# A hybrid transformer layer on one core: the gates take two or three turns over the contraction, the later conditioning keeps a pace, and the modulation moves to ScalarE

## The chip, the cores and the metric

The kernel runs on one core of a Trainium2 chip. The metric is the time of one execution in device microseconds (us); lower is better. A core has TensorE (PE in the profile) for matmuls and transposes, VectorE (DVE) and ScalarE (ACT) for work on whole tiles, GpSimd (POOL) for small things, and SyncE (SP), whose queue issues the loads from memory. Each engine runs its own instructions in order and waits on semaphores for the others.

## The reference, cut to what matters

256 latent tokens and 256 context tokens of width 2048 are normalised, modulated by the conditioning, and go through one input projection. Two attentions follow; their outputs are weighted by sigmoid gates, projected, and added to the tokens; a gated feed-forward network ends the layer.

```
sh1, sc1, g1, sh2, sc2, g2 = ada_terms(cond_lat, w_ada, b_ada)       # silu(c) @ w_ada + b_ada
ctx_terms = ada_terms(cond_ctx, w_ada, b_ada)
z_ctx = modulate(rms_norm(ctx, norm1_g), ctx_terms[0], ctx_terms[1])  # h * (1 + scale) + shift
ctx_proj = z_ctx @ w_in[:, :1088]          # MLA kv latent 512 | rope key 64 | GQA k 256 | GQA v 256
z_lat = modulate(rms_norm(x, norm1_g), sh1, sc1)
lat_proj = z_lat @ w_in                    # the same 1088 | MLA q latent 768 | GQA q 1024 | gates 2 x 2048
x = x + g1 * attend_and_merge(lat_proj, keys)    # sigmoid(g_a) * (o_a @ w_br_a) + sigmoid(g_b) * (o_b @ w_br_b), then @ w_out
x = x + g2 * conv_ffn(modulate(rms_norm(x, norm2_g), sh2, sc2))
```

## The kernel before, in words

**Products.** All large products are float32 in two parts: a high part, rounded, and a low part, the rest. `mm3` takes three matmuls for one product: high by high, high by low, low by high. Weights come by SP's queue, 1 MB at a time, into a ring of four buffers (`raw`). ACT casts the high part (`hi`), DVE subtracts to get the low one (`lo`), and three buffers hold such units; `take()` keeps two of them ahead of TensorE.

**Who goes when.** TensorE's order is the order in which the program is written. Side work stands in "lanes", generators that a modelled clock lets run a step at a time when the main line yields: class `Pace` adds up the modelled TensorE time, lets the modelled backlog of DVE, ACT and DMA run down with it, and runs a lane's next step when the backlogs are under that lane's limit. `Engine` holds the modelled cost of an instruction. `finish(lane)` runs what is left of a lane at once, whatever the backlog. On DVE and ACT the instructions then stand in an order that follows the model.

**Input projection.** The 16 tiles of 128 rows of the contraction are taken in parts (`CHUNKS`). For each part `gemv_chunk` makes the shift and scale from `w_ada` on TensorE (matmuls `raw,cs`, an ACT copy, a few transposes, three small DVE instructions on `md`), and `make_z` the modulated tokens: the high part by one ACT instruction, the modulated value by a DVE `tensor_scalar` in place (`sX<-sX,md`), the low part by a DVE subtraction. Latent tokens are `ZL`, context tokens `ZC`. Then blocks of columns are multiplied: a (MLA kv latent, rope key), b (GQA k and v), c (MLA q latent), d (GQA q) and the gates 0 to 3 of 1024 columns each; a and b take both kinds of token, the others latents alone. A block's result is copied out of PSUM by ACT the first time and added to what stands there by DVE (`sG<-bank,sG`, `sK<-bank,sK`) every later time. Two strings, `ORDER0` and `ORDERM`, set the order of blocks in a part; in the last two parts the gates come last and take both parts in one turn.

**Side work in this stretch.** `lane_ctx` prepares the context tokens in part 0. `ada_rest`, the later conditioning, makes shift, scale and gate for the rest of the layer on DVE: eight sums of 16 steps `acc<-raw,cs,acc`, each step half of a 1 MB load of `w_ada`; it may take 32 loads at first, then 48, then 64. In the last part `prep_b` rotates GQA keys and queries on DVE (`scratch<-sK,sY`, then `sK<-scratch`), turns them by transposes on TensorE (`ident,sK`) and splits them. It is finished when gate 0 is through. Then `lane_heads_b` (GQA attention) and `lane_latents` run as lanes under the gates 1 to 3, and `lane_latents` is finished after gate 3, ahead of `q_up`. It consists of `prep_cq`, `prep_ckv` (sums of squares by matmuls with `ones`, a reciprocal root on POOL, its spread over rows by `ident,rr`, and a scaling of four tiles on DVE) and `prep_kpe` (the rope key: transposes of `acc_pe`, a rotation on `kr` and `kt`, then eight transposes `ident,scratch`).

**Later stages.** q_up, the GQA projection, MLA attention, its projection, `w_out`, then the residual with the gate `g1`, which `ada_rest` makes (`acc,ones` matmuls and an ACT copy), the normalised tokens by transposes, up and down projection.

Of the kernel before, what the change touches and what calls it, by code (L numbers as in the profile page):

```python
# [29 lines left out]
CHUNKS = (2, 3, 3, 4, 4)  # L30
# [4 lines left out]
ORDER0, ORDERM, CTX_AT = "cd012ab3", "abcd0123", 2  # L35
# [3 lines left out]
REST_CI, REST_AFTER, REST_DMA = 1, 6.0, 6.0  # L39
GAPS = (0.0, 4.0, 10.0, 14.0, 14.0)  # L40
# [10 lines left out]
class Pace:  # L51
# [26 lines left out]
    def tick(self):  # L78
        if self.busy:
            return  # L80
        self.busy = True
        moved = True
        while moved:
            moved = False
            for lane in list(self.lanes):
                gen, ready, limit, dma, _ = lane
                if self.pe < ready or self.left["dve"] > limit or self.left["act"] > limit or self.left["dma"] > dma:
# [31 lines left out]
class Engine:  # L119
# [31 lines left out]
def _build(tc, nc, es, a):  # L151
# [139 lines left out]
    def lane_tables():  # L291

        r = slot("X0", [P, 4, P])
# [124 lines left out]
    def make_z(ci, cnd):  # L418
        kt0, nk = starts[ci], CHUNKS[ci]
        md = mods[ci]  # L420
        zt = slot(("ZL", "ZC")[cnd] + str(ci % 2), [P, 2, nk, T], F32R)
        zs[ci][cnd] = zt
        c = slice(cnd * T, (cnd + 1) * T)
        for k in range(nk):
# [8 lines left out]
    zs = [[None, None] for _ in CHUNKS]  # L433
# [7 lines left out]
    def ada_rest():  # L441
        for vname, v, gslot in (("sh2", 3, None), ("sc2", 4, None), ("g1", 2, "K1"), ("g2", 5, "Y0")):
            for sec in range(2):
# [4 lines left out]
                for j0 in range(0, 16, 2):  # L448
                    r = load(w_ada[:, j0:j0 + 2, c0:c0 + 1024], [P, 2, 1024])
                    taken_raws[0] += 1  # L450
                    for j in range(2):
# [3 lines left out]
                        else:  # L455
                            DVE.scalar_tensor_tensor(out=acc, in0=r[:, j, :], scalar=cs[:, j0 + j, 0:1], in1=acc,
                                                     op0=ALU.mult, op1=ALU.add)
                        yield 0.0
# [37 lines left out]
    rest = ada_rest()  # L496
# [46 lines left out]
    def zk(zt, k):  # L543
        return zt[:, 0, k, :], zt[:, 1, k, :]

# [3 lines left out]
    def block_a(ci):  # L549
        kt0, nk, z = starts[ci], CHUNKS[ci], zs[ci]  # L550
# [4 lines left out]
        for kk in range(nk):  # L555
            wh, wl = take()
            for n in range(5):
                m = 128 if n < 4 else 64
                for cnd in range(2):
                    zh, zl = zk(z[cnd], kk)  # L560
                    mm3(ps[n][:m, cnd * T:(cnd + 1) * T], wh[:, n * P:n * P + m], wl[:, n * P:n * P + m],
                        zh, zl, kk == 0 and cnd == 0, kk == nk - 1)
# [3 lines left out]
    def block_b(ci):  # L566
        kt0, nk, z = starts[ci], CHUNKS[ci], zs[ci]
# [3 lines left out]
        for k0, kn in halves(nk):  # L571
            wh, wl = take()
            for k in range(kn):
                kk = k0 + k
                for t in range(4):
                    c = slice((t % 2) * P, (t % 2 + 1) * P)
                    zh, zl = zk(z[t // 2], kk)
                    mm3(ps[t], zh[:, c], zl[:, c], wh[:, k, :], wl[:, k, :], kk == 0, kk == nk - 1)
# [3 lines left out]
    def block_c(ci):  # L582
        kt0, nk, z = starts[ci], CHUNKS[ci], zs[ci]
# [3 lines left out]
        for kk in range(nk):  # L587
            group_T(ps, take(), zk(z[0], kk), kk == 0, kk == nk - 1)
# [3 lines left out]
    def block_d(ci):  # L592
        kt0, nk, z = starts[ci], CHUNKS[ci], zs[ci]
# [3 lines left out]
        for kk in range(nk):  # L597
            wh, wl = take()
            zh, zl = zk(z[0], kk)
            for t in range(2):  # L600
                c = slice(t * P, (t + 1) * P)
                for n in range(2):
                    d = slice(n * 512, (n + 1) * 512)
                    mm3(ps[2 * t + n], zh[:, c], zl[:, c], wh[:, d], wl[:, d], kk == 0, kk == nk - 1)
# [9 lines left out]
    def block_g(cis, g):  # L614
# [4 lines left out]
        for i, (ci, k) in enumerate(ks):  # L619
            group_T(ps, take(), zk(zs[ci][0], k), i == 0, i == len(ks) - 1)  # L620
# [24 lines left out]
    def weights():  # L645
# [11 lines left out]
        for ci in range(nch):  # L657
            for b in order(ci):
                yield from wb(ci) if b == "b" else win(ci, *cols[b])
        for g in "0123":  # L660
            for ci in (nch - 2, nch - 1):
                yield from win(ci, *cols[g])
# [59 lines left out]
    for ci in range(nch - 1):  # L722
# [4 lines left out]
        if ci == REST_CI:  # L727
            pace.add(rest, after=REST_AFTER, limit=REST_LIM, dma=REST_DMA, prio=9)
        if ci == 2:
            pace.add(lane_tables(), after=5.0, limit=1.0, prio=8)  # L730
        for i, b in enumerate(order(ci)):
# [8 lines left out]
            run(block_g([ci], int(b)) if b in "0123" else {"a": block_a, "b": block_b, "c": block_c, "d": block_d}[b](ci))  # L740
# [4 lines left out]
    zo, zl_ = f"ZL{nch % 2}", f"ZL{last % 2}"  # L745
# [27 lines left out]
    def prep_b():  # L773
# [25 lines left out]
        qbh = slot("X0", [P, 4, 512], F32R)  # L799
# [192 lines left out]
    pace.limit(rest, REST_LIM_B)  # L992
# [6 lines left out]
    for g in range(4):  # L999
        run(block_g([last - 1, last], g))  # L1000
# [54 lines left out]
    pace.limit(rest, REST_LIM_Q)  # L1055
# [24 lines left out]
    obh = slot(zl_, [P, H, T], F32R)  # L1080
# [17 lines left out]
    oah = slot(zl_, [P, H, T], F32R)  # L1098
# [66 lines left out]
    pace.limit(rest, REST_LIM_A)  # L1165
# [4 lines left out]
    pace.limit(rest, REST_LIM_W)  # L1170
# [309 lines left out]
```

## Time and profile before

| | before |
|---|---|
| median of 3 runs | 1548.19 us (1545.66 to 1550.21) |
| the profiled execution | 1547.03 us, its span 1545.2 us |
| TensorE busy | 1506.1 us (97%) |
| DVE busy | 1103.3 us (71%) |
| ACT busy | 768.9 us (50%) |
| loads and stores | 350.44 MB, 227 GB/s in the mean |

The span is the part of the execution in which the profiler saw the core's engines at work; 1.8 us lie around it. Busy time is time in which an engine has an instruction under way; a TensorE matmul starts before the one ahead of it has ended, so its busy time says little about its speed, and its idle time (39 us) is what a wait costs. A wait is written behind the instruction that it held up, with the engine that ended it. Line L140 is the call in `Engine` through which all DVE and ACT work goes, L210 the matmul of `mm`, L219 the transpose, L398 the matmul of `gemv_chunk`.

### The profile page before, as it was taken

How to read it: one execution, taken by the hardware profiler on the slowest of the kernel's cores; microseconds unless marked ns; L12 is line 12 of the kernel's file. 1: busy time of each engine (PE TensorE's matmuls, PEld its weight loads, DVE VectorE, ACT ScalarE, POOL GpSimd, SP SyncE). 2: the span in 40 equal slices, each digit the busy share in tenths (PEclk: the TensorE clock that was granted, in tenths of full speed). 3: DMA queues.
4: the chain of work that ended last, by engine and by line, in shares of the span. 5: the costliest groups of instructions: out<-in, count | busy, mean ns of one | idle time of the engine just before them, and what ended most of it. 6: DMA issues, size and time to landing. Idle time of an engine off the chain costs nothing.

```text
span 1545.2 us, 23200 instructions
## 1 busy us (share of the span) xinstructions
PE 1506.1 (97%) x9361; PEld 1321.8 (86%) x9361; DVE 1103.3 (71%) x1553; ACT 768.9 (50%) x1145; POOL 14.2 (1%) x23
## 2 busy tenths in 40 slices
PE   6999999999999999999989999999999999999997
PEld 5788888899998988998879888888888888888885
DVE  3457686798778888698878989667666666555556
ACT  4634242355775446643446545555545555444444
POOL 0000000010000000000000000000000000000000
PEclk9999999999999999999989999999999999999998
DMA  9779888755346885478967878655555565555552
GB/s 360 243 251 331 286 313 292 257 181 191 110 134 208 280 286 187 146 275 310 351 225 257 295 256 294 215 182 181 186 192 191 167 204 180 194 199 196 195 195 78
DMA packets 123676, 350.44 MB, mean 227 GB/s; under 512 B 6718, under 2 KB 20264, under 8 KB 117040
## 3 DMA queue, kind: packets, MB, share of 16 engines
q1 hardware_dynamic: 123568, 348.96, 65.2%
q8 instruction: 73, 1.20, 0.3%
q14 instruction: 35, 0.29, 0.1%
HBM read 346.84 MB, written 2.10 MB: 226 GB/s over the span
## 4 chain that ended last, share of the span: by engine, by line
PE 92%; DVE 3%; DMA 3%; ACT 1%; issue 0%; SPq 0%; ACTq 0%; POOLq 0%; POOL 0%; DVEq 0%
PE bank L210 89%; PE bank L219 2%; PE bank L398 2%; DMA raw<-in_w_ada 1%; DMA raw<-in_w_in 1%; DVE scratch L140 1%; DVE lo L140 1%; DVE sK L140 1%; DMA sK<-in_x 0%; DVE sX L140 0%; ACT scratch L140 0%; DVE acc L140 0%; SPq L392 0%; ACT sK L140 0%; DVE sG L140 0%
## 5 line engine op out<-in xcount | busy, mean ns | idle before, releaser
L140 DVE TENSOR_TENSOR lo<-raw,hi 128x1024 fp32r<-128x1024 f32 (+2 forms) x463 | 548.5, 1188 | 302.6 <-ACT hi L140 300.7
L140 ACT CAST hi<-raw 128x1024 fp32r<-128x1024 f32 (+2 forms) x463 | 471.7, 1021 | 579.0 <-PE bank L210 471.1
L210 PE MATMUL bank<-sZL,hi 128*128 128x256 f32 (+2 forms) x2528 | 592.9, 316 | 3.0 <-ACT hi L140 2.5
L210 PE MATMUL bank<-sZL,lo 128*128 128x256 f32 (+1 forms) x1648 | 467.5, 284 | 0.6 <-DVE lo L140 0.6
L210 PEld LDWEIGHTS bank<-sZL,hi 128*128 128x128 f32 (+1 forms) x2528 | 422.2, 192 | 44.5 <-issue 7.5
L210 PEld LDWEIGHTS bank<-sZL,lo 128*128 128x128 f32 (+1 forms) x1648 | 315.6, 191 | 1.1 <-DVE lo L140 1.1
L210 PE MATMUL bank<-sX,hi 128*128 128x512 f32 (+1 forms) x896 | 287.6, 367 | 0.0
L210 PE MATMUL bank<-hi,sZC 128*128 128x512 f32 (+1 forms) x816 | 261.1, 383 | 0.0
L210 PE MATMUL bank<-sX,lo 128*128 128x256 f32 x704 | 198.0, 281 | 0.0
L210 PEld LDWEIGHTS bank<-sX,hi 128*128 128x128 f32 x896 | 164.8, 189 | 30.2 <-issue 0.5
L210 PEld LDWEIGHTS bank<-hi,sZC 128*128 128x128 f32 x816 | 152.6, 188 | 29.8
L140 DVE SCALAR_TENSOR_TENSOR acc<-raw,cs,acc 128x1024 f32<-128x1024 f32 x120 | 153.6, 1280 | 11.4 <-DMA raw<-in_w_ada 10.5
L210 PEld LDWEIGHTS bank<-sX,lo 128*128 128x128 f32 x704 | 133.4, 189 | 0.5 <-issue 0.5
L210 PE MATMUL bank<-lo,sZC 128*128 128x512 f32 (+1 forms) x344 | 131.5, 382 | 0.3 <-DVE lo L140 0.3
L210 PEld LDWEIGHTS bank<-lo,sZC 128*128 128x128 f32 x344 | 64.7, 188 | 13.2 <-DVE lo L140 0.7
L140 DVE TENSOR_TENSOR sK<-bank,sK 128x512 f32<-128x512 f32 (+1 forms) x92 | 60.0, 685 | 8.8 <-PE bank L210 7.5
L210 PE MATMUL bank<-hi,sZL 128*128 128x512 f32 x192 | 63.4, 393 | 0.1
L140 ACT COPY scratch<-bank 128x256 f32<-128x256 f32 (+3 forms) x92 | 35.1, 392 | 36.5 <-PE bank L210 23.1
L210 PE MATMUL bank<-sZC,hi 128*128 128x256 f32 x256 | 50.4, 284 | 1.4 <-DVE sZC L140 1.4
L210 PE MATMUL bank<-lo,sX 128*128 128x512 f32 x128 | 50.1, 392 | 0.9 <-DVE lo L140 0.9
L210 PE MATMUL bank<-hi,sX 128*128 128x512 f32 x128 | 50.3, 393 | 0.0
L140 DVE TENSOR_TENSOR sG<-bank,sG 128x512 f32<-128x512 f32 x64 | 41.9, 683 | 6.3 <-PE bank L210 6.3
(202 smaller groups left out, 1405.7 us busy)
## 6 DMA issues: line engine op xcount, KB each, us to landing
raw<-in_w_up SPq DMA_DIRECT2D x88, 1024.0 KB, 5.1
raw<-in_w_ada SPq DMA_DIRECT2D x82, 1024.0 KB, 6.7
raw<-in_w_down SPq DMA_DIRECT2D x44, 1024.0 KB, 5.8
raw<-in_w_in SPq DMA_DIRECT2D x37, 1024.0 KB, 5.1
raw<-in_w_out SPq DMA_DIRECT2D x16, 1024.0 KB, 7.5
raw<-in_w_ada SPq DMA_DIRECT2D x16, 768.0 KB, 5.1
raw<-in_w_br_b SPq DMA_DIRECT2D x8, 1024.0 KB
raw<-in_w_br_a SPq DMA_DIRECT2D x8, 1024.0 KB, 8.1
```

Source lines behind the costliest of these rows:

```text
L140: return f(*args, **kw)
L210: PE.matmul(out, lhsT, rhs, start=start, stop=stop, skip_group_check=True)
L219: PE.transpose(out, src, ident[:n, :n])
L398: PE.matmul(ps[32 * g:32 * g + 32, :cols], cs[:, j0 + jj, :], w[:, jj, :], start=j0 + j == 0, stop=j0 + j == 14, skip_group_check=True)
```

## The change

The parts become 2, 2, 4, 4, 4 tiles. The order of blocks is written out for each part, and a gate is multiplied over all parts since its last turn: gates 0 and 1 in three turns (part 0; 1 and 2; 3 and 4), gates 2 and 3 in two (0 to 2; 3 and 4), where each took four. So that a gate can reach back, the modulated latents of earlier parts are kept in four slots (`ZL0`, `ZL1`, `X0`, `ZL0` again), and some other tiles change their slot. In `make_z` the in-place modulation becomes a second ACT instruction, in all but the latents of part 0. `ada_rest` starts in part 2, not in part 1, and later in it (`REST_AFTER`), and is paced: as long as it has made fewer than one step for each `REST_EVERY` us of modelled TensorE time, its limit is raised to `REST_LATE`. The modelled costs become larger.

```diff
-CHUNKS = (2, 3, 3, 4, 4)
+CHUNKS = (2, 2, 4, 4, 4)
-ORDER0, ORDERM, CTX_AT = "cd012ab3", "abcd0123", 2
+ORDERS, CTX_AT = ("cd01ab", "abcd", "abcd2301", "abcd", "bdca0123"), 2
-REST_CI, REST_AFTER, REST_DMA = 1, 6.0, 6.0
-GAPS = (0.0, 4.0, 10.0, 14.0, 14.0)
+REST_CI, REST_AFTER, REST_DMA, REST_EVERY, REST_LATE = 2, 30.0, 6.0, 4.4, 2.6
+GAPS = (0.0, 4.0, 5.0, 14.0, 14.0)
...
             if self.key == "act":
-                c = 0.1 + 0.85e-3 * n
+                c = 0.17 + 0.86e-3 * n + (0.19 if "accum_out" in kw else 0.0)
...
             elif name in ("tensor_scalar", "tensor_copy"):
-                c = 0.06 + 0.58e-3 * n
+                c = 0.13 + 0.66e-3 * n
             else:
-                c = 0.06 + 1.05e-3 * n
+                c = 0.14 + 1.06e-3 * n
...
-        pace.tensor(n * 0.417e-3 if rhs.dtype == F32R else max(n, 256) * 1.67e-3)
+        pace.tensor(0.013 + n * 0.417e-3 if rhs.dtype == F32R else max(n, 256) * 1.67e-3)
...
-            ACT.activation(zt[:, 0, k, :], x, AF.Identity, bias=s2, scale=s1)
-            DVE.tensor_scalar(out=x, in0=x, scalar1=s1, scalar2=s2, op0=ALU.mult, op1=ALU.add)
-            DVE.tensor_sub(zt[:, 1, k, :], x, zt[:, 0, k, :].bitcast(F32))
+            hi, lo = zk(ci, cnd, k)
+            ACT.activation(hi, x, AF.Identity, bias=s2, scale=s1)
+            if ci == 0 and cnd == 0:
+                DVE.tensor_scalar(out=x, in0=x, scalar1=s1, scalar2=s2, op0=ALU.mult, op1=ALU.add)
+            else:
+                ACT.activation(x, x, AF.Identity, bias=s2, scale=s1)
+            DVE.tensor_sub(lo, x, hi.bitcast(F32))
...
+    def paced(limit):
+        def now():
+            if rest_from[0] is None:
+                rest_from[0] = pace.pe
+            return max(limit, REST_LATE) if rest_steps[0] < (pace.pe - rest_from[0]) / REST_EVERY else limit
+
+        return now
...
-    def order(ci):
-        if ci == nch - 1:
-            return "bdca"
-        o = ORDER0 if ci == 0 else ORDERM
-        return "".join(x for x in o if x in "abcd") if ci == nch - 2 else o
+    def gate_parts(ci, g):
+
+        done = [c for c in range(ci) if g in ORDERS[c]]
+        return list(range(done[-1] + 1 if done else 0, ci + 1))
...
-    pace.limit(rest, REST_LIM_B)
+    pace.limit(rest, paced(REST_LIM_B))
...
-        run(block_g([last - 1, last], g))
+        run(block_g(gate_parts(last, str(g)), g))
```

**Order, first place: the end of the gates, ahead of q_up, on TensorE.** `sZL` by `hi` or `lo` are matmuls of a gate, `sK,sX` those of a GQA head, the rows with `ones`, `rr`, `acc_pe` and `scratch` belong to `lane_latents`, `sZC` is q_up. Before:

```order
L210 MATMUL bank<-sZL_2968,lo 128x256
L219 MATMUL bank<-ident,acc_pe 128x64 x4
L210 MATMUL bank<-sZL_2968,hi 128x256 x2
L210 MATMUL bank<-sZL_2968,lo 128x256
...
L219 MATMUL bank<-ident,scratch 128x128 x8
L210 MATMUL bank<-sZC_4647,hi 128x256
```

And in the change:

```order
L215 MATMUL bank<-sZL_2772,lo 128x256
L215 MATMUL bank<-sK_4991,sX_3339 128x256 x12
L215 MATMUL bank<-ones,scratch 128x1 x8
L215 MATMUL bank<-ident,rr 128x128 x4
L224 MATMUL bank<-ident,acc_pe 128x64 x4
L224 MATMUL bank<-ident,scratch 128x128 x8
L215 MATMUL bank<-sZC_5050,hi 128x256
```

Before, the rows with `ones` and `rr` stand far ahead of this place, and sixteen rows of gate matmuls lie between the last two transposes of the lane. In the change the whole lane from its sums on stands behind the last gate matmul, with nothing between. What DVE has there in the change, from the root's spread (`rr`) to what the last transposes read (`sZL` and `sK` are low parts, `sK_604` to `sK_607` the four tiles that are scaled):

```order
L145 COPY rr<-st 128x128 x2
L145 TENSOR_TENSOR sZL_5474<-sY_4130,sZL_5473 128x256
...
L145 COPY kr<-bank 128x256
L145 SCALAR_TENSOR_TENSOR scratch<-sK_604,vec,scratch 128x512
L145 SCALAR_TENSOR_TENSOR scratch<-sK_605,vec,scratch 128x512
L145 SCALAR_TENSOR_TENSOR scratch<-sK_606,vec,scratch 128x512
L145 TENSOR_TENSOR sK_5102<-scratch,sK_5099 128x512
...
L145 TENSOR_TENSOR kt_5127<-kr,tabA 128x64
...
L145 CAST scratch<-kr 128x4x64 x2
L145 TENSOR_TENSOR scratch<-kr,scratch 128x4x64
```

Before, DVE had the scaling of those four tiles ahead of `COPY kr<-bank` among the low parts of the gates' weights.

**Second place: the end of gate 0 in the last set, on TensorE.** `ident,sK_710` are the transposes of the keys, `ident,sK_311` those of the queries. Before, the last of them:

```order
L219 MATMUL bank<-ident,sK_311 128x128 x4
L210 MATMUL bank<-sZL_2968,hi 128x256 x2
...
L219 MATMUL bank<-ident,sK_311 128x128 x12
L210 MATMUL bank<-sZL_2189,hi 128x256 x2
```

And in the change:

```order
L215 MATMUL bank<-sZL_2772,lo 128x256
L224 MATMUL bank<-ident,sK_710 128x128 x8
L224 MATMUL bank<-ident,sK_311 128x128 x16
L215 MATMUL bank<-sX_1702,hi 128x256 x2
```

All 24 transposes now stand behind gate 0 in one piece. On DVE the rotations of the queries (`sK_311<-scratch` ends one; `sX_3761` and `sX_3763` are low parts of turned keys and queries) stand in the change as follows:

```order
L145 TENSOR_TENSOR sX_3761<-bank,sX_3761 128x512 x2
L145 TENSOR_TENSOR sK_311<-scratch 128x512
L145 TENSOR_TENSOR scratch<-sK_311,sY_102 128x8x32 x2
L145 TENSOR_TENSOR scratch<-sK_311,sY_102 128x512
L145 TENSOR_TENSOR sX_3763<-bank,sZL_3762 128x512
L145 TENSOR_TENSOR sK_311<-scratch 128x512
L145 TENSOR_TENSOR sX_3763<-bank,sZL_3762 128x512
L145 TENSOR_TENSOR scratch<-sK_311,sY_102 128x8x32 x2
L145 TENSOR_TENSOR lo<-raw,hi 128x1024
L145 TENSOR_TENSOR sK_311<-scratch 128x512
```

Ahead of the last of these `sK_311<-scratch` DVE has 58 steps `acc<-raw,cs,acc` where it had 27 before, 8 additions `sG<-bank,sG` where it had 32, and 2 `tensor_scalar` on `sX` where it had 32.

**Third place: from part 1 to part 2, on ScalarE.** `scratch<-bank` is the copy of the conditioning's sums, `sZL` and `sZC` by `md` the high parts, `sX` by `md` the modulation in place, which stood on DVE before. In the change:

```order
L145 COPY scratch<-bank 128x512
L145 ACTIVATE sZL_1055<-sX_105,md 128x256 x2
L145 ACTIVATE sX_105<-sX_105,md 128x256 x2
L145 ACTIVATE sZL_1055<-sX_105,md 128x256 x2
L145 ACTIVATE sX_105<-sX_105,md 128x256 x2
L145 ACTIVATE sZC_1068<-sX_105,md 128x256 x2
L145 ACTIVATE sX_105<-sX_105,md 128x256 x2
L145 ACTIVATE sZC_1068<-sX_105,md 128x256 x2
L145 ACTIVATE sX_105<-sX_105,md 128x256 x2
```

On TensorE block b of part 1, the transposes of the conditioning and the first product of part 2 follow each other there with no gate between; before, gates 0 to 3 stood between the parts, gate 3 alone between parts 0 and 1.

## Rows read from the trace of the kernel before

**Rows 1.** The page's first part: busy us, share of span, instructions of each engine.
```profile
PE 1506.1 (97%) x9361; PEld 1321.8 (86%) x9361; DVE 1103.3 (71%) x1553; ACT 768.9 (50%) x1145; POOL 14.2 (1%) x23
```

**Rows 2.** TensorE's waits: line waited for, us in total, times, longest.
```profile
PE bank L219 <- DVE scratch L140: 9.6, 3, 5.9
...
PE bank L210 <- DVE lo L140: 2.5, 4, 0.9
...
PE bank L210 <- DVE sZC L140: 1.4, 1, 1.4
```

**Rows 3.** Windows: length, busy of PE, PEld, DVE, ACT, POOL; clock, DMA share, GB/s.
```profile
130.00:350.00 220.00, 219.65 (x1562) 193.35 (x1561) 172.74 (x257) 83.14 (x145) 5.98 (x3) 1.00 0.77 270
```

**Rows 4.** Another such window, the fullest in loads.
```profile
750.00:775.00 25.00, 25.00 (x112) 20.74 (x111) 22.73 (x20) 8.75 (x9) 0.00 (x0) 1.00 0.97 370
```

**Rows 5.** DVE's groups by form: count, busy us, mean ns, idle before.
```profile
L140 DVE TENSOR_TENSOR lo<-raw,hi 128x1024 fp32r<-128x1024 f32 x417 | 508.4, 1223 | 277.1 <-ACT hi L140 275.3
L140 DVE SCALAR_TENSOR_TENSOR acc<-raw,cs,acc 128x1024 f32<-128x1024 f32 x120 | 153.6, 1280 | 11.4 <-DMA raw<-in_w_ada 10.5
L140 DVE TENSOR_TENSOR sG<-bank,sG 128x512 f32<-128x512 f32 x64 | 41.9, 683 | 6.3 <-PE bank L210 6.3
...
L140 DVE TENSOR_SCALAR sX<-sX,md 128x256 f32<-128x256 f32 x32 | 12.1, 409 | 2.0 <-ACT sZL L140 2.0
```

**Rows 6.** Timeline between parts 0 and 1: start, us, instruction, count, [idle before]: DVE, ACT.
```profile
83.87 0.17 DVE L140 SCALAR_TENSOR_TENSOR md<-md,vec 128x6 f32<-128x6 f32 x1
...
85.91 0.75 DVE L140 TENSOR_TENSOR sZL<-sX,sZL 128x256 fp32r<-128x256 f32 x2
...
84.46 1.58 ACT L140 ACTIVATE sZL<-sX,md 128x256 fp32r<-128x256 f32 x3
```

**Rows 7.** Timeline, ends of the query rotations and their transposes: DVE, PE.
```profile
340.23 1.36 DVE L140 TENSOR_TENSOR scratch<-sK,sY 128x256 f32<-128x256 f32 x3
341.51 0.69 DVE L140 TENSOR_TENSOR sK<-scratch 128x512 f32<-128x512 f32 x1
...
353.32 0.67 DVE L140 TENSOR_TENSOR sK<-scratch 128x512 f32<-128x512 f32 x1
...
363.18 1.28 DVE L140 TENSOR_TENSOR sX<-bank,sX 128x512 fp32r<-128x512 f32 x2
...
370.81 1.47 PE L219 MATMUL bank<-ident,sK 128*128 128x128 f32 x12
```

**Rows 8.** Timeline of the latents' lane under the last gates: PE, POOL, DVE.
```profile
454.39 0.95 PE L210 MATMUL bank<-ones,scratch 128*128 128x1 f32 x8
...
455.71 1.01 POOL L239 TENSOR_TENSOR st<-st,mhalf 128x4 f32<-128x4 f32 x1 [17.94 <-ACT hi L140]
...
456.76 0.36 DVE L140 COPY rr<-st 128x128 f32<-128x128 f32 x2 [1.21 <-POOL st L239]
...
460.46 2.07 DVE L140 SCALAR_TENSOR_TENSOR scratch<-sK,vec,scratch 128x512 f32<-128x512 f32 x3
462.45 1.29 DVE L140 TENSOR_TENSOR sK<-scratch,sK 128x512 fp32r<-128x512 f32 x2
...
472.80 0.42 DVE L140 TENSOR_TENSOR kt<-kr,tabA 128x64 f32<-128x64 f32 x3
...
477.05 1.06 PE L219 MATMUL bank<-ident,scratch 128*128 128x128 f32 x8 [2.52 <-DVE scratch L140]
```

**Rows 9.** Timeline at the end of w_out: PE, DVE.
```profile
776.47 1.88 PE L210 MATMUL bank<-acc,ones 128*128 128x512 f32 x4
784.25 0.69 PE L219 MATMUL bank<-ident,scratch 128*128 128x128 f32 x2 [5.90 <-DVE scratch L140]
...
778.15 0.69 DVE L140 TENSOR_TENSOR scratch<-bank,sK 128x512 f32<-128x512 f32 x1 [1.70 <-ACT sK L140]
...
783.11 0.69 DVE L140 TENSOR_TENSOR sK<-sK,scratch 128x512 f32<-128x512 f32 x1
```

**Rows 10.** The clock at that end, in the windows' columns.
```profile
782.00:793.00 11.00, 7.08 (x30) 6.19 (x31) 8.42 (x19) 4.91 (x9) 1.11 (x2) 0.53 0.30 101
```

More of the change, by code (lines that the diff above doesn't have):

```diff
@@ L291, in lane_tables @@
     def lane_tables():
-        r = slot("X0", [P, 4, P])
+        r = scratch([P, 4, P])
         POOL.memset(r, 0.0)
@@ L420, in make_z @@
         md = mods[ci]
-        zt = slot(("ZL", "ZC")[cnd] + str(ci % 2), [P, 2, nk, T], F32R)
-        zs[ci][cnd] = zt
+        if cnd:
+            zc[ci] = slot(f"ZC{ci % 2}", [P, 2, nk, T], F32R)
+        elif kt0 % 4 == 0:
+            zl.append(slot(ZSLOTS[kt0 // 4], [P, 2, 4, T], F32R))
         c = slice(cnd * T, (cnd + 1) * T)
@@ L427, in make_z, with zk @@
             s1, s2 = md[:, 1, k, cnd:cnd + 1], md[:, 0, k, cnd:cnd + 1]
-            ACT.activation(zt[:, 0, k, :], x, AF.Identity, bias=s2, scale=s1)
-            DVE.tensor_scalar(out=x, in0=x, scalar1=s1, scalar2=s2, op0=ALU.mult, op1=ALU.add)
-            DVE.tensor_sub(zt[:, 1, k, :], x, zt[:, 0, k, :].bitcast(F32))
-            yield 0.0
-    zs = [[None, None] for _ in CHUNKS]
+            hi, lo = zk(ci, cnd, k)
[5 more added lines that the diff above has]
+            DVE.tensor_sub(lo, x, hi.bitcast(F32))
+            yield 0.0
+    ZSLOTS = ("ZL0", "ZL1", "X0", "ZL0")
+    zl, zc = [], {}
+    def zk(ci, cnd, k):
+        if cnd:
+            return zc[ci][:, 0, k, :], zc[ci][:, 1, k, :]
+        kt = starts[ci] + k
+        return zl[kt // 4][:, 0, kt % 4, :], zl[kt // 4][:, 1, kt % 4, :]
     s2col = cst.tile([P, KT], F32, name="s2col")
@@ L549, in block_a @@
     def block_a(ci):
-        kt0, nk, z = starts[ci], CHUNKS[ci], zs[ci]
+        nk = CHUNKS[ci]
         if ci == 0:
@@ L559, in block_a @@
                 for cnd in range(2):
-                    zh, zl = zk(z[cnd], kk)
+                    zh, zl_ = zk(ci, cnd, kk)
                     mm3(ps[n][:m, cnd * T:(cnd + 1) * T], wh[:, n * P:n * P + m], wl[:, n * P:n * P + m],
-                        zh, zl, kk == 0 and cnd == 0, kk == nk - 1)
+                        zh, zl_, kk == 0 and cnd == 0, kk == nk - 1)
             yield
@@ L566, in block_b @@
     def block_b(ci):
-        kt0, nk, z = starts[ci], CHUNKS[ci], zs[ci]
+        nk = CHUNKS[ci]
         if ci == 0:
@@ L582, in block_c @@
     def block_c(ci):
-        kt0, nk, z = starts[ci], CHUNKS[ci], zs[ci]
+        nk = CHUNKS[ci]
         if ci == 0:
@@ L587, in block_c @@
         for kk in range(nk):
-            group_T(ps, take(), zk(z[0], kk), kk == 0, kk == nk - 1)
+            group_T(ps, take(), zk(ci, 0, kk), kk == 0, kk == nk - 1)
             yield
@@ L592, in block_d @@
     def block_d(ci):
-        kt0, nk, z = starts[ci], CHUNKS[ci], zs[ci]
+        nk = CHUNKS[ci]
         if ci == 0:
@@ L657, in weights @@
         for ci in range(nch):
[L658 to L662, printed above, removed]
+            for b in ORDERS[ci]:
+                if b == "b":
+                    yield from wb(ci)
+                else:
+                    for c in gate_parts(ci, b) if b in "0123" else [ci]:
+                        yield from win(c, *cols[b])
         for u in range(2):
@@ L727, in _build @@
         if ci == REST_CI:
-            pace.add(rest, after=REST_AFTER, limit=REST_LIM, dma=REST_DMA, prio=9)
+            pace.add(rest, after=REST_AFTER, limit=paced(REST_LIM), dma=REST_DMA, prio=9)
         if ci == 2:
             pace.add(lane_tables(), after=5.0, limit=1.0, prio=8)
-        for i, b in enumerate(order(ci)):
+        for i, b in enumerate(ORDERS[ci]):
             if ci == 0 and i == CTX_AT:
@@ L739, in _build @@
                 lc = None
-            run(block_g([ci], int(b)) if b in "0123" else {"a": block_a, "b": block_b, "c": block_c, "d": block_d}[b](ci))
+            run(block_g(gate_parts(ci, b), int(b)) if b in "0123" else {"a": block_a, "b": block_b, "c": block_c, "d": block_d}[b](ci))
         while ci + 1 not in mods:
@@ L744, in _build @@
     last = nch - 1
-    zo, zl_ = f"ZL{nch % 2}", f"ZL{last % 2}"
+    zo, zn = "ZL1", "ZL0"
     run(block_b(last))
@@ L1053, in lane_q @@
             yield 0.0
-    pace.limit(rest, REST_LIM_Q)
+    pace.limit(rest, paced(REST_LIM_Q))
     run(q_up(0))
@@ L1163, in lane_a @@
             yield from head_a(2 * pr + par)
-    pace.limit(rest, REST_LIM_A)
+    pace.limit(rest, paced(REST_LIM_A))
     la = [pace.add(lane_a(i), limit=LIM_ATT, prio=1 + i) for i in range(2)]
@@ L1169, in _build @@
     hold[0] = 48
-    pace.limit(rest, REST_LIM_W)
+    pace.limit(rest, paced(REST_LIM_W))
     mgh = [slot(f"X{i}", [P, 8, T], F32R) for i in range(2)]
```

23 lines of the change are left out of this document (12 added, 11 removed).

## The prediction, made before the changed kernel ran

> **What bounds the kernel now.** I read the page's engine totals first, then TensorE's waits, the windows by stage, the groups of DVE, and last the timeline where the order of instructions changes. TensorE is busy for 1506.1 us [rows 1] of a span of 1545.2; it bounds the kernel, and only some 39 us of idling can be won at all. The list of its waits shows how few they are: transposes that read a DVE result wait 9.6 us in three places, the worst 5.9; products that wait for a low part 2.5 us in four [rows 2]. Through most of the projection it stands almost never: 219.65 of 220 us busy from 130 to 350 us, at full clock, with DVE busy 172.74 and loads at 270 GB/s [rows 3]. There, whatever makes DVE or ACT cheaper wins nothing by itself. A change can gain only at the few joints where TensorE waits, and it can lose at any place where side work stops having matmuls over it.
>
> **The change part by part.** The matmuls stay the same in number; what moves is which work lies over which.
>
> *Fewer gate additions, modulation off DVE.* 24 of 64 additions of 683 ns go, 16.4 us, and 30 of 32 `tensor_scalar` of 409 ns, 12.3 us [rows 5]. They lie under matmuls [rows 3], so I count them at nothing. ACT takes 30 instructions more; three high parts in a row take it 1.58 us, 0.5 each [rows 6], 15 us in all, also mostly under matmuls, but not at the joints, next.
>
> *Joint of parts 0 and 1.* Gate 3 covered it; now the first product of part 1 follows the transposes of the conditioning. Behind these come three small `md` instructions (0.17 each, 0.6 with their gaps), then on ACT two latent high parts, two in-place modulations, two context high parts and two more modulations, 0.5 each. The first tile's low part for context needs the seventh, 0.6+3.5, and a subtraction of 0.4 (0.75 for two) [rows 6]: 4.5 us. TensorE has for it part of a conditioning vector and the first latent products, some 1.5 to 2. I take +2.5 (2 to 3).
>
> *Joint of parts 1 and 2.* The same with four tiles; and the ACT copy of the conditioning's sums stands ahead, 0.6. The first context high part is the ninth ACT instruction and its low part needs the eleventh: 0.6+0.6+11x0.5+0.4 = 7.1, and two low parts of weights wait in the same DVE queue, which brings it to 7.85. TensorE covers 3 of it: +4.85. The low bound is 0, if the conditioning is far enough ahead. Here a page speaks against the edit: the Trainium skill, ScalarE: Activation LUTs, section Rules for kernel authors, gives simple arithmetic such as `mul` and `add` to VectorE rather than ScalarE. The rows agree on one instruction (409 ns on DVE [rows 5], 0.5 spaced on ACT [rows 6]); by that rule the joint would cost about 3.1, since two engines would share the chain.
>
> *Rest of the front.* The context tokens lose two `tensor_scalar` ahead of their low part: the 1.4 us wait for `sZC` [rows 2] falls by 0.7. Waits of 0.9 at part 1's loads and low parts (the longest of [rows 2]) go with the block order. After the joints' waits the clock may sit at its lower level: +1.2 (0 to 2.3, the price below). Front: 2.5+4.85-0.7-0.9+1.2 = **+7** (0 to 9).
>
> *Heads, at the end of gate 0 of the last set.* Here the pacing acts. Ahead of the last query rotation DVE gets 31 more steps of the later conditioning (31x1.28 = 39.7 us), 7 low parts more (8.5), and 24 additions and 30 `tensor_scalar` fewer (16.4+12.3) [rows 5]: about 20 us more. Before, the last rotation ended at 354.0 and its transposes came at 370.81 without a wait [rows 7]: 17 us of slack. That is eaten, and the order shows it: all 24 transposes stand behind gate 0. In the least case DVE is not late at all and only runs what needs the keys' transposes: low parts 1.28, then the end of one rotation and two full ones of 1.36+0.69 without what stands ahead, and a low part of weights, 1.2 [rows 5, 7]: at least 7.3 us, under which TensorE has 1 us of transposes: +6.3. If DVE is the remaining 3 to 6 us late, up to +12. I take +8, and +1.5 for the clock: **+9.5** (6.3 to 13). Behind the transposes gate 1 stands in TensorE's queue.
>
> *Latents, at the end of the gates.* Before, the lane lay under gate matmuls and only its last transposes waited, 2.52 us [rows 8]. Now it stands behind the last gate. In a row: 12 matmuls of a head 1.4, the sums with `ones` 1.0, one DVE instruction 0.2, POOL 1.2 (its 1.01 and the way), together 3.8. Then DVE: four `rr` copies 0.7, five low parts of 0.35 between, `kr` 0.4, four scalings (2.07 for three) 2.7, four low parts (1.29 for two) 2.5, six `kt` (0.42 for three) 0.8, three more low parts 1.0, an addition 0.6, the casts and the last subtraction 0.8 [rows 5, 8]: 11.3. With waits between TensorE and DVE at the third `rr` and at `kr`, about 1.3: 16.4 us (15.5 to 17.5). TensorE's own work in it is 3.5: 12.9 idle, less the 2.52 of before: +10.4 (9.5 to 12.5). POOL's queue holds nothing else here, and q_up stands behind the wait. The clock's price: after the wait of 5.90 us and two short ones at the end of w_out the granted clock was 0.53 over 11 us, that is 10.3 of them at 1.2 GHz [rows 9, 10]; some 4 us of matmuls then ran at half speed, about 2 us lost. After the 2.52 us wait it did not fall. For 13 us of standing I take +2.3 (0 to 4): **+12.7** (10 to 16.5).
>
> *End of w_out.* The gate `g1` was made last: its four matmuls (1.88) stand behind w_out, and the residual starts at 778.15 and ends at 783.8, four pairs of multiplication and addition [rows 9]. In the change `g1` is made 14 us of TensorE earlier, so three pairs (1.35 each) run while w_out's last banks are under way: **-4.0** (-3 to -6, with the clock).
>
> *The pace itself.* 31 steps more, half a load of 1.05 MB each, are 16.3 MB on the 59.4 MB of those 220 us [rows 3]: 344 GB/s. Over 25 us the queue has carried 370 at a share of 0.97 [rows 4]; by the 270 at 0.77 of this stretch a share of 0.97 would be 340. I count 0; at a share of 0.93, 326 GB/s, TensorE waits for weights: 75.7/0.326-220 = +12.
>
> Sum, against the execution's own 1547.03: 1547.0+7+9.5+12.7-4.0 = **1572**. That execution lies 1.2 us below the median of the runs, which changes nothing here. The bounds of the terms one by one give 1562 to 1580 for this case.
>
> **The rivals.** *Only the latents' joint stays.* The 58 steps may run early enough, DVE having lost 28.7 us of work in the same stretch, and the conditioning be ahead at the front. Then only the transposes' own chain shows: 1547+12.7-4 = 1556. For it: DVE has 47 us free in those 220. Against: the order, which puts a rotation behind the transposes in any case.
> *The loads bind as well.* 344 GB/s are asked for over 220 us, with no room left at the stretch's own rate; it adds 12: 1572+12 = 1584. For it: loads of 1 MB for the sums stand in the same ring of four as the weights. Against: 370 in rows 4.
> *The joints cost little, no change.* If the scheduler's place of an instruction is later than its true moment, each joint costs 2 to 3 us; they add up to 6 and the end of w_out gives 4: 1549. Against: the chain of the latents has its least length from durations, not from places.
> *Faster.* The end of w_out is relieved, with the clock's fall there gone as well (-6), and the joints must cost less than 1.5 us together. It needs the lanes to be through before the gates end, in spite of the order: 1541. It decides from there: joints above 6 us in all end it.
> *The pacing does nothing* (the limits do not let one step more in) is excluded by the order, which has 58 for 27.
>
> **How the numbers follow.** The likeliest case, all three joints, has 0.52; only the latents' joint 0.20; loads as well 0.17; no change 0.05; faster 0.06. The predicted time is the first's, 1572. Up to the loads' case and down to the second it reaches from 1553 to 1586, leaving out the last two cases and the far end of the third. A change of 0.3%, 4.6 us, is about what a measurement of this kernel can tell from none. So: faster 0.06, same 0.05, slower 0.89; within the likeliest, 1562 to 1580.
>
> **What the changed profile would show.** Right: a wait for DVE of 10 us or more at the last `ident,scratch` transposes ahead of q_up, or two that add up to it; waits of 6 us or more at `ident,sK` behind gate 0; some 5 us more for `sZL` and `sZC` in the first 150 us; the wait of 5.9 at the end of w_out down to 2; most of 130 to 350 us with loads above 320 GB/s. Wrong: the front joints without a wait (the conditioning ran ahead); waits for low parts all through 130 to 350 us (loads or DVE bind); full clock right behind the long waits, which would take 5 us off; and above all a latents' joint under 5 us, by which the whole forecast would fall.

## The result, and the profile after

| | before | after |
|---|---|---|
| median, five runs each | 1548.57 us (1545.66 to 1550.21) | 1576.62 us (1573.93 to 1579.10) |
| the profiled execution, its span | 1547.03, 1545.2 us | 1576.62, 1574.8 us |

The change makes the kernel slower: 1.0181 times the time of before [1.0169 to 1.0193], 28 us. The forecast was 1572, in a range that holds the result. The engine totals on the page of after (as [rows 1]):

```profile
PE 1510.9 (96%) x9361; PEld 1327.2 (84%) x9361; DVE 1081.9 (69%) x1498; ACT 785.5 (50%) x1174; POOL 14.6 (1%) x23
```

VectorE has 21 us less to do, and the same 9361 matmuls end 29.6 us later. TensorE is idle for 1574.8-1510.9 = 63.9 us, where it was 1545.2-1506.1 = 39.1 [rows 1]: 24.8 of the 29.6 are new waits. Most stand at what the prediction calls joints, places where one run of matmuls ends and the next needs work of other engines that nothing covers. TensorE's waits in the trace of after, as [rows 2]:

```profile
PE bank L224 <- DVE scratch L145: 13.0, 3, 8.6
PE bank L224 <- DVE sK L145: 7.0, 3, 3.3
PE bank L403 <- DMA raw<-in_w_ada: 5.9, 7, 1.6
...
PE bank L215 <- DVE sZC L145: 5.1, 3, 3.0
PE bank L215 <- DVE lo L145: 3.3, 7, 0.8
...
PE bank L215 <- DVE rr L145: 1.9, 1, 1.9
...
PE bank L215 <- DVE sZL L145: 1.5, 2, 1.1
```

The timeline says where they stand (start, us, instruction, and in brackets the wait ahead of it). The joint of parts 0 and 1, that of parts 1 and 2, the heads at 390, the latents from 502, and the end of w_out, on TensorE:

```profile
79.02 0.39 PE L215 MATMUL bank<-sZL,hi 128*128 128x256 f32 x1 [1.06 <-DVE sZL L145]
...
80.99 0.39 PE L215 MATMUL bank<-sZC,hi 128*128 128x256 f32 x1 [1.06 <-DVE sZC L145]
...
115.74 0.38 PE L215 MATMUL bank<-sZC,hi 128*128 128x256 f32 x1 [0.80 <-ACT sZC L145]
117.18 0.48 PE L215 MATMUL bank<-sZC,hi 128*128 128x256 f32 x1 [1.06 <-DVE sZC L145]
...
390.15 1.59 PE L224 MATMUL bank<-ident,sK 128*128 128x128 f32 x7 [3.32 <-DVE sK L145]
392.98 0.45 PE L224 MATMUL bank<-ident,sK 128*128 128x128 f32 x1 [1.24 <-DVE sK L145]
395.89 1.76 PE L224 MATMUL bank<-ident,sK 128*128 128x128 f32 x7 [2.47 <-DVE sK L145]
...
502.28 1.17 PE L215 MATMUL bank<-ones,scratch 128*128 128x1 f32 x8 [0.96 <-DVE scratch L145]
505.31 2.38 PE L215 MATMUL bank<-ident,rr 128*128 128x128 f32 x8 [1.87 <-DVE rr L145]
...
516.93 1.94 PE L224 MATMUL bank<-ident,scratch 128*128 128x128 f32 x8 [8.62 <-DVE scratch L145]
...
819.03 0.44 PE L224 MATMUL bank<-ident,scratch 128*128 128x128 f32 x2 [2.93 <-DVE scratch L145]
```

The rotation that the last query transposes need ends on DVE at 395.16+0.68, and they start at 395.89: at each of the three waits TensorE follows one `sK<-scratch`. The chain that sets the end of the stretch from 500 to 520 us, in order of time (start, us, what):

```profile
501.60 1.10 POOL rqa L244
...
503.99 1.02 POOL st L244
...
505.31 2.38 PE bank L215 x8
...
508.77 1.98 DVE scratch L145 x3
510.75 1.80 DVE sK L145 x3
...
516.93 1.94 PE bank L224 x8
```

Each link is short and none lies beside gate matmuls; TensorE is 8.56 us busy in these 20. Windows of after: at the heads, the latents, the stretch of [rows 3], and from the first up product to the end; the last row is that stretch of before:

```profile
385.00:405.00 20.00, 12.97 (x84) 12.08 (x83) 17.13 (x30) 5.72 (x9) 0.00 (x0) 0.74 0.38 145
500.00:520.00 20.00, 8.56 (x48) 7.85 (x47) 14.31 (x41) 14.46 (x31) 2.41 (x3) 0.58 0.06 23
130.00:350.00 220.00, 215.68 (x1491) 187.76 (x1484) 165.72 (x194) 91.22 (x157) 4.24 (x2) 0.99 0.86 311
823.30:1574.80 751.50, 740.41 (x4031) 641.34 (x4031) 514.95 (x683) 389.70 (x542) 1.10 (x2) 0.99 0.59 205
```
```profile
788.50:1545.20 756.70, 745.99 (x4031) 642.72 (x4031) 514.62 (x683) 389.28 (x542) 1.10 (x2) 0.99 0.59 203
```

Ahead of the up projection the same 5330 matmuls are busy for 1510.9-740.41 = 770.5 us, where they took 1506.1-745.99 = 760.1: 10.4 us more. In the windows of both long joints the granted clock is 0.74 and 0.58 in the mean, between its levels of 1.2 and 2.4 GHz. In the stretches at the lower level ahead of the up projection TensorE is busy for 30.2 us in after and for 8.3 in before; half of the difference, 11.0, is what the slower clock takes, close to the 10.4. The up projection and what follows takes 5.2 us less, with the same matmuls and the same clock (last section). So 29.6 is 24.8 of waits, 10.4 of slower matmuls, and -5.6 of faster ones.

### The profile page after: what moved, and what is told of

It reads as the page before. It is cut to its first block, busy times and chain, and to the rows that moved or that the text cites. A ratio compares the mean times of both kernels' runs of the same rounds, so it can differ in the third digit from the quotient of the medians.

```text
span 1574.8 us, 23126 instructions
## 1 busy us (share of the span) xinstructions
PE 1510.9 (96%) x9361; PEld 1327.2 (84%) x9361; DVE 1081.9 (69%) x1498; ACT 785.5 (50%) x1174; POOL 14.6 (1%) x23
## 4 chain that ended last, share of the span: by engine, by line
PE 85%; DVE 6%; DMA 5%; ACT 2%; issue 1%; SPq 0%; POOL 0%; ACTq 0%; POOLq 0%; DVEq 0%
PE bank L215 81%; DMA raw<-in_w_ada 2%; PE bank L224 2%; PE bank L403 2%; DVE lo L145 2%; DMA raw<-in_w_out 1%; DVE acc L145 1%; DVE sK L145 1%; DVE scratch L145 1%; DMA raw<-in_w_in 1%; ACT hi L145 1%; DVE sX L145 1%; ACT scratch L145 0%; DMA sK<-in_x 0%; DVE sG L145 0%
## 5 line engine op out<-in xcount | busy, mean ns | idle before, releaser
L215 PE MATMUL bank<-sZL,hi 128*128 128x256 f32 (+1 forms) x2184 | 527.6, 319 | 4.1 <-ACT hi L145 2.5
L215 PE MATMUL bank<-sZL,lo 128*128 128x256 f32 (+1 forms) x1476 | 418.6, 284 | 0.6 <-DVE lo L145 0.6
L215 PEld LDWEIGHTS bank<-sZL,hi 128*128 128x128 f32 x2184 | 369.4, 192 | 44.0 <-issue 5.4
L215 PE MATMUL bank<-sX,hi 128*128 128x512 f32 (+1 forms) x1240 | 349.9, 342 | 0.0
L215 PEld LDWEIGHTS bank<-sZL,lo 128*128 128x128 f32 (+1 forms) x1476 | 283.2, 192 | 1.0 <-DVE lo L145 0.8
L215 PE MATMUL bank<-sX,lo 128*128 128x256 f32 (+1 forms) x876 | 246.8, 282 | 0.0
L215 PEld LDWEIGHTS bank<-sX,hi 128*128 128x128 f32 x1240 | 219.1, 190 | 29.2 <-issue 1.3
L215 PEld LDWEIGHTS bank<-sX,lo 128*128 128x128 f32 (+1 forms) x876 | 166.6, 190 | 0.5 <-issue 0.5
L145 ACT COPY scratch<-bank 128x256 f32<-128x256 f32 (+2 forms) x92 | 34.8, 392 | 40.8 <-PE bank L215 21.4
L215 PEld LDWEIGHTS bank<-sZC,hi 128*128 128x128 f32 x256 | 40.8, 192 | 6.9 <-DVE sZC L145 5.7
```

## The experiments

**Theory:** the chains at heads and latents are a row of links between TensorE, VectorE and POOL. They cost what they last wherever nothing else stands for TensorE between the links, and it is the pace of the later conditioning (start, limit, modelled costs) that pushed the lanes to the ends of the gates; the front joints are the turns of the gates, which leave them without cover. **Rivals:** VectorE is merely late, so that a lane released earlier ends earlier; the modulation on ScalarE is what makes the joints long; TensorE waits for the loads.

Ratios are to the kernel before, measured on the same chip (medians there 1547.57 to 1549.15), with the 95% interval; differences in us are of medians.

**One lane's limit each.** The first raises the latents' limit in after, the second that of the heads' preparation.

```diff
-... LIM_ATT, LIM_LAT = ... 3.0, 1.3
+... LIM_ATT, LIM_LAT = ... 3.0, 3.0
```

> The change with one number altered: the limit of the latents' lane goes from 1.3 to 3.0, so that its sums, its spread and its last transposes lie under the gates 1 to 3 again; the heads stay where they are. Uncovered joints as the cause: the 11.5 us of waits from the sums to the last transposes shrink to 3 or less, and some 3 to 4 us of half clock behind them go too: 1562 to 1567 us. The loads or VectorE as the limit: VectorE has the same work, the wait turns up at low parts or at the GQA heads, 1573 or more.

```diff
-    lb = pace.add(prep_b(), limit=1.2)
+    lb = pace.add(prep_b(), limit=4.0)
```

> The change with one number altered: the limit of the lane that rotates and turns the GQA heads goes from 1.2 to 4.0; 16 of its 24 transposes then lie under gate 0, the last 8 still stand behind it. Uncovered joints as the cause: of 7.0 us of waits there and some 3 us of half clock, 5 to 8 go: 1568 to 1572 us. VectorE behind with its work (the pace): the rotations come as late as before in time, and the waits stay at 7 or move to the low parts of gate 0: 1575 to 1578.

Latents: 1578.15 us (1572.80 to 1586.74, 4 runs), 1.0196 [1.0151 to 1.0240], no gain, a miss: the time is in the rival's range. The lane's last wait fell from 8.62 to 0.79, but the waits stand at its head now, on TensorE:

```profile
450.94 1.87 PE L215 MATMUL bank<-ones,scratch 128*128 128x1 f32 x8 [5.12 <-DVE scratch L145]
...
487.94 1.05 PE L215 MATMUL bank<-ones,scratch 128*128 128x1 f32 x8 [3.26 <-DVE scratch L145]
```

and on DVE, in the same run, the additions that the first of them waits for:

```profile
447.21 1.28 DVE L145 SCALAR_TENSOR_TENSOR acc<-raw,cs,acc 128x1024 f32<-128x1024 f32 x1
448.40 0.69 DVE L145 TENSOR_TENSOR scratch<-scratch 128x512 f32<-128x512 f32 x1
449.00 1.28 DVE L145 TENSOR_TENSOR sK<-bank,sK 128x512 fp32r<-128x512 f32 x2
450.20 0.68 DVE L145 TENSOR_TENSOR scratch<-scratch 128x512 f32<-128x512 f32 x1
```

The limit moves TensorE's instruction ahead; what it needs stands on DVE behind a step of the conditioning and low parts, which did not move. In this trace TensorE is also busy for 42.8 us at the lower clock ahead of the up projection, where it was 30.2. Only 4 us of the difference lie behind these two waits (10.7 for 6.6); most of the rest is in the first 240 us, which the edit did not touch. Behind equal waits the clock falls in one execution and not in another: behind one of 1.06 us at 82 us here, but not behind the same one at 81 in after. Heads: 1566.83 (1564.24 to 1568.86, 4), 1.0122 [1.0105 to 1.0138], 9.8 us less than after, a little more than forecast: the 7.0 us at `ident,sK` are gone, with some of the clock (20.2 us busy at the lower level for 30.2); in the traces 2.4 us of the gain lie in the up projection (last section).

**Both limits at once**, 4.0 for either lane.

> The change with two limits altered: the heads' lane 1.2 to 4.0, the latents' lane 1.3 to 4.0. With the latents' limit alone the waits of the chain stayed at 11 us, since VectorE came late to the sums; with the heads early as well VectorE has room under gates 1 to 3. Uncovered joints as the cause: both joints go, 1576.6-9.8-8.9 and 2 to 4 us of half clock: 1552 to 1558 us. VectorE's order as the limit, whatever stands on TensorE: the heads' 10 us are won and the latents' waits stay: 1564 to 1569.

1568.90 us (1563.12 to 1571.46, 4), 1.0126 [1.0106 to 1.0146], as the heads alone. That is a miss: the theory's case was 1552 to 1558, and the time is that of VectorE's order as the limit. The latents still wait in two places, 7.9 us in all where after has 11.45:

```profile
426.16 2.61 PE L215 MATMUL bank<-ident,rr 128*128 128x128 f32 x8 [3.31 <-DVE rr L145]
...
458.05 1.94 PE L224 MATMUL bank<-ident,scratch 128*128 128x128 f32 x8 [4.58 <-DVE sK L145]
```

That VectorE is merely late falls with it: released far earlier, the chain keeps most of its waits. The clock takes back what was won: ahead of the up projection TensorE is idle 4.8 us less than with the heads alone and busy 6.4 us more.

**The chain spread under later matmuls.** After with the heads' limit at 4.0; the latents' lane is run only to the query latents ahead of q_up, and its rest goes as a lane under q_up and the GQA projection.

```diff
-    finish(ll)
+    while "ql" not in A:
+        next(ll)
...
     finish(lq[1])
+    finish(ll)
```

> The change with the heads' limit at 4.0 (1566.8 us by itself) and the latents' lane no longer finished after the gates: q_up needs only its scaled query latents, so the rest of the lane, from the second sums on, runs as a lane under q_up and the GQA projection. Uncovered joint as the cause: the 10.5 us of waits from the spread to the last transposes and some 3 us of half clock go: 1552 to 1557 us. VectorE's latency, wherever the chain stands: the waits come back at the same instructions among q_up's matmuls, 1562 or more.

1557.16 us (1547.81 to 1559.68, 7), 1.0040 [1.0019 to 1.0061], at the edge of the theory's case and 9.7 less than with the heads alone (12.7 by the ratios, since these runs spread widely). In its trace, an execution of 1551.07 us, the links wait for nothing any more, the spread, the rope key and the last transposes in turn:

```profile
500.45 1.44 PE L215 MATMUL bank<-ident,rr 128*128 128x128 f32 x8
...
555.38 0.46 PE L224 MATMUL bank<-ident,acc_pe 64*128 64x64 f32 x4
...
561.63 1.03 PE L224 MATMUL bank<-ident,scratch 128*128 128x128 f32 x8
```

Waits of 1.21 and 0.30 us are left near by, at transposes of the later conditioning and at a head's product. It is the place of the links, not the limit, that decides.

**The pace undone** in after: start, limit and modelled costs as before, all else changed.

```diff
-REST_CI, REST_AFTER, ... = 2, 30.0, ...
+REST_CI, REST_AFTER, ... = 1, 6.0, ...
...
-            return max(limit, REST_LATE) if rest_steps[0] < (pace.pe - rest_from[0]) / REST_EVERY else limit
+            return limit
```

> The change without its pace: the later conditioning starts in part 1, its limit is never raised, the modelled costs are those of before; parts, turns of the gates, slots and ScalarE's modulation stay. Uncovered joints as the cause, the pace being what pushed the lanes behind the gates: heads and latents stand as in the kernel before, 7.0+8.9 us of waits and some 7 us of half clock go, the 2.7 us won at the end of w_out go back, the joints between the parts stay: 1553 to 1560 us. The turns or ScalarE's modulation as the cause: 1568 or more.

1556.49 us (1555.21 to 1557.49, 4), 1.0055 [1.0040 to 1.0070], 20 us less than after, as the theory had it. No wait is left at the heads, and the latents' last transposes wait 2.52, as in [rows 8]:

```profile
479.48 0.74 PE L224 MATMUL bank<-ident,scratch 128*128 128x128 f32 x5 [2.52 <-DVE scratch L145]
```

From 260 to 380 us, where the lanes' work should have been done, the windows differ in DVE (fourth number) and in the loads. After, and then this run:

```profile
260.00:380.00 120.00, 119.05 (x811) 108.70 (x810) 114.21 (x148) 52.77 (x110) 5.98 (x3) 1.00 0.87 304
```
```profile
260.00:380.00 120.00, 120.00 (x829) 112.15 (x829) 99.30 (x146) 56.08 (x114) 6.19 (x3) 1.00 0.59 201
```

With the pace DVE has 6 us free of 120, without it 21. That alone does not decide: with the chain spread, in the run above, DVE is busy for 113.38 us of the same window, and the chains are hidden. The start, the limit and the modelled costs were not tried apart.

**The gates' turns.** Gates 2 and 3 take a turn at the ends of parts 0 and 1 again, over the joints, so that each gate has three; the second kernel has the pace undone as well.

```diff
-ORDERS, CTX_AT = ("cd01ab", "abcd", "abcd2301", "abcd", "bdca0123"), 2
+ORDERS, CTX_AT = ("cd01ab2", "abcd3", "abcd0123", "abcd", "bdca0123"), 2
```

> The change with another order of blocks: gate 2 behind b in part 0, gate 3 at the end of part 1, all four gates in part 2; each gate takes three turns. So the joints of parts 0 and 1 and of parts 1 and 2 lie under a gate again. Uncovered joints: the waits of 2.1 and 3.6 us there go with 1 to 2 us of half clock, 8 additions more cost nothing: 1568 to 1573. The conditioning's loads as the cause of the front's time: the waits move to the loads, 1575 or more.

> The change with its pace undone, as in the run before, and with gates 2 and 3 over the joints of the first parts; three turns for each gate and ScalarE's modulation stay. Uncovered joints: the 9 us that were left over the kernel before shrink by 5 to 7: 1548 to 1552. Three turns for four, 16 additions fewer, worth something of their own: below 1546. ScalarE's modulation or the slots as the cost: 1555 or more.

Turns alone: 1567.94 us (1566.02 to 1571.54, 4), 1.0128 [1.0110 to 1.0145], 8.7 less than after, just below the theory's case. The waits at both front joints are gone; TensorE waits 9.3 us for loads of the conditioning (5.9 in after), 13.3 at the latents. At the heads only 0.87 is left, though the transposes stand behind gate 0 as in after: VectorE was through there. So the order's place on TensorE alone doesn't make that wait, and much of these 8.7 us was won at the heads, not in the front. Both: 1546.55 (1544.83 to 1549.55, 10), 0.9987 [0.9977 to 0.9998]. Pace (20 us) and turns (another 9.9), undone in this order, are the whole loss; what remains of the change, the parts, the slots, modulation on ScalarE and fewer gate additions, is together worth 2 us (0.3 to 3.6).

**Modulation on VectorE**, in after.

```diff
-            if ci == 0 and cnd == 0:
+            if True:
```

> The change with the in-place modulation on VectorE again for all parts, nothing else altered. Uncovered joints as the cause: the chains of the joints between the parts get shorter by 1 to 3 us in all, since two engines share them, and the rest stays: 1573 to 1576 us. ScalarE's modulation as the main cost of the change: 1565 or less. VectorE as the limit of the stretch: 30 instructions of 0.41 us more make it 1580 or more.

1582.25 us (1580.37 to 1586.21, 4), 1.0226 [1.0208 to 1.0244], 5.6 more than after, a miss in sign: the case of VectorE as the limit. The waits of the joint of parts 1 and 2 fall from 3.6 to 2.0 us, but those at the heads rise from 7.0 to 10.4, the first line below; the window at the heads shows DVE busy for 23.85 of 25 us:

```profile
PE bank L224 <- DVE sK L145: 10.4, 4, 4.2
```
```profile
380.00:405.00 25.00, 14.59 (x98) 13.42 (x98) 23.85 (x38) 6.88 (x10) 0.00 (x0) 0.73 0.68 250
```

Here 12.3 us more on DVE [rows 5] are not hidden, with DVE as full as that. The rule of the Trainium skill in the prediction (ScalarE: Activation LUTs, Rules for kernel authors: VectorE for `mul` and `add`) holds for the joint and not for the whole. Another page of the Trainium skill fits the whole, Perfetto Trace Analysis, section Optimizing Scalar/DVE Operations: where DVE is saturated, giving some of its work to ScalarE may make sense. DVE's 114.21 of 120 us in after agree.

**`g1` earlier in before:** `REST_LIM_W`, the conditioning's limit during w_out, 2.2 for 1.4.

> The kernel before with one number altered: the limit of the later conditioning under the MLA projection and w_out goes from 1.4 to 2.2, so that the second half of g1 stands 48 matmuls, some 9 us, ahead of w_out's end. If the late g1 held up the residual: three pairs of residual work go under w_out, 3 to 4 us less: 1544 to 1546. If something else held it up: 1547 to 1549.

1548.66 us (1545.58 to 1554.70, 12), 1.0001 [0.9990 to 1.0013]: nothing, a miss. The wait at the end of w_out fell as in after, 2.93 for 5.90. TensorE's waits in this trace show where it went:

```profile
PE bank L219 <- DVE scratch L140: 6.9, 3, 2.9
...
PE bank L210 <- DVE lo L140: 5.2, 6, 1.9
```

2.7 us less at `scratch` and 2.7 more at low parts [rows 2], one of 1.91 at 690.91. Two steps of the conditioning stand on DVE at 680.58, some 9 us ahead of that low part; that they are what delays it was not shown.

**Together.** The first takes the spread chain and the turns with the pace kept; the second has the pace of before and three turns for each gate, as the kernel of 1546.55 us, the rest of the latents' lane under the first half of q_up, and its last transposes held back longer.

```diff
-        yield 2.5
+        yield 8.0
...
-    finish(ll)
+    while "ql" not in A:
+        next(ll)
...
     run(q_up(0))
+    finish(ll)
```

> The change with its pace kept and all three kinds of joints covered: heads' limit 4.0, the latents' chain under q_up, gate 2 behind part 0's blocks and gate 3 behind part 1's. If the joints are all that the change costs: 1544 to 1550 us, within 0.3% of the kernel before, with 2 to 3 us of waits for the conditioning's loads left over. If the pace costs by itself, by loads and by VectorE's work: 1554 or more.

> The change with its pace undone and the gates over the first joints (1546.6 us, the fastest so far), and the last transposes of the latents' lane moved under q_up. If the 2.5 us wait there, which the kernel before has too, costs its length and a stretch of half clock: 1542 to 1544.5. If it is given back at the next wait: 1546 to 1547.5.

First: 1551.03 us (1547.54 to 1556.17, 12), 1.0018 [1.0003 to 1.0032], between its two cases: with the joints covered 4.5 us are left over the kernel without the pace (1546.55). TensorE still waits 6.3 us for the conditioning's loads (1.8 in before) and 5.5 for low parts (2.5). Second: 1542.48 (1539.49 to 1547.91, 12), 0.9963 [0.9950 to 0.9977], as forecast if the 2.5 us count: faster than both kernels, where pace and turns alone give 0.9987. Its trace has no wait at all from 380 to 520 us; the row of its windows at the latents:

```profile
470.00:490.00 20.00, 20.00 (x163) 18.79 (x162) 17.71 (x37) 13.54 (x25) 0.00 (x0) 1.00 0.77 246
```

## Why the prediction came out, point by point

| term | forecast | after less before |
|---|---|---|
| joint of parts 0 and 1 | +2.5 | +2.1 |
| joint of parts 1 and 2 | +4.85 | +3.6 |
| context tokens | -0.7 | +0.7 |
| part 1's loads and low parts | -0.9 | -0.9 |
| heads, without the clock | +8 | +7.0 |
| latents, without the clock | +10.4 | +8.9 |
| end of w_out | -4.0 | -2.7 |
| loads of the conditioning, front | 0 | +3.0 |
| other waits | 0 | +2.7 |
| clock | +5.0 | +10.4 |
| up projection on | 0 | -5.2 |

- **Joints.** Right in place and kind. The second was costed 1.25 too dear; 1.0 of its 3.6 is a load, not ScalarE's chain.
- **Context tokens.** Wrong in sign. The two `tensor_scalar` do cost what was taken (with them back on DVE the wait for `sZC` is 3.63, without them 2.98), but TensorE, which waits 0.88 less at the transposes ahead, comes to that product some 2 us earlier against DVE's work, and the wait rose from 1.43.
- **Heads.** The least case held: VectorE was busy but no more than its own chain late, 7.0 against 6.3 to 13. That all 24 transposes stand behind gate 0 was read as the cause; with the turns of the gates restored they stand there too and wait 0.87. The place made the wait possible, but VectorE had to be late as well: the wait goes with the pace undone, with the turns restored and with the lane released earlier, each by itself.
- **Latents.** 0.96+1.87+8.62 = 11.45 us of waiting, less 2.52: +8.9 for 10.4. The chain went much as summed, 14.65 us from the sums to the last transposes for 15.0. This step carried the forecast, and it held.
- **End of w_out.** 2.93 and two short waits, 4.8 in all where 7.6 stood (5.90 of it in [rows 9]): -2.7. That the time is won was wrong in one respect: in before the same relief alone won nothing, since low parts took it back. In after the low parts from 650 to 800 us make TensorE wait 2.4 us, where before had 0.9 ahead of its end of w_out: half of the gain is taken back there too.
- **Modulation and fewer additions at nothing.** Nearly right where DVE has room: with pace and turns undone all that is left of the change is worth 2 us. In after DVE has none, and the modulation put back on it costs 5.6.
- **Loads.** The rival in which they bind did not come. The stretch of [rows 3] moved 311 GB/s, not 344, since the last rotation to which the 31 steps were counted stands at 395, not 353; 24 of them lie in the stretch. TensorE lost 4.3 of those 220 us, 3.4 of them to three loads of the front's own conditioning, a price that the prediction did not have.
- **Clock.** The mis-sized term. It was set at 5.0 from the end of w_out and the joints' waits; the matmuls ahead of the up projection took 10.4 us more. In after the granted clock was also below full at 55 to 65 us, 115 to 125 and 220 to 230 (0.83 each), behind waits of 1 to 3 us. TensorE was busy at the lower level for 9.0 us there, 6.5 at the heads and 6.6 at the latents; half of that is 4.5, 3.3 and 3.3, where the forecast had 1.2, 1.5 and 2.3. That the clock did not fall behind the 2.52 us wait of before was no guide to waits of that length.

The signs came as named, the first of them as three waits that add up to 11.45, the fourth as 2.93 for 2. The bounds of the terms, added up, give 1557 to 1583, not the 1562 to 1580 written beside the sum; the result lies in both. The idle terms are within 1.5 us each; a clock twice as dear and 5.7 us of waits that were not counted are partly made up by 5.2 given back where nothing was changed. That these make up for each other was not forecast, so it is by luck that 1576.6 for 1572 is a little nearer than the terms are.

## What to carry to other kernels

Side work that is a chain of short links over several engines costs most of its length at any place where the next matmul stands behind its last link. Here raising the limit of the latents' lane moved only TensorE's end of it, and stretching the chain under matmuls that come later hid it. Before a background task is given a pace, look at the stretch in which it runs for the engine that the chains need: with 21 of 120 us free on VectorE they were hidden as they stood, with 6 they were not, until the heads were released earlier and the latents' links spread. And allow for the clock behind each new wait: here 24.8 us of waits came with 10.4 us of slower matmuls, a price that was not the same in each execution.

## What was not expected

The stretch from the first up product to the end is 5.2 us shorter in after, though its instructions are the same. Groups by form in 250 us of the up projection (count, busy us, mean ns), before and after; and after again, from 880 to 1030 us:

```profile
L210 PE MATMUL bank<-sX,hi 128*128 128x512 f32 x357 | 126.7, 399 | 0.0
```
```profile
L215 PE MATMUL bank<-sX,hi 128*128 128x512 f32 x370 | 128.8, 391 | 0.0
```
```profile
L215 PE MATMUL bank<-sX,hi 128*128 128x512 f32 x214 | 76.4, 401 | 0.0
```

At a granted clock of 1.00 a pair of products, 512 and 256 columns, starts every 0.3533 us in before and every 0.3469 in after's 250 us. In after both spacings occur: it has that of before up to the last four matmuls of the later conditioning, and the shorter one behind them, in the middle of a block:

```profile
1031.93 0.40 PE L215 MATMUL bank<-sX,hi 128*128 128x512 f32 x1
...
1032.28 1.88 PE L215 MATMUL bank<-acc,ones 128*128 128x512 f32 x4
...
1034.35 0.39 PE L215 MATMUL bank<-sX,hi 128*128 128x512 f32 x1
```

A block takes its PSUM banks once, at its start, so it is not the bank. In 250 us chosen like these the five kernels without the pace (before, the two with it undone, `g1` earlier, the fastest) have 399 ns, the eight with it 391. Three of the eight (the latents' limit alone, the heads' limit alone, the chain spread) have the shorter spacing through the whole up projection, which makes it another 2 us shorter. So the 20 us that undoing the pace gave back are already less some 6 (757.7 us from the first up product on, for 751.5). What makes the two spacings was not found, and that part of the accounting stays open.
